# Six w_down blocks rounded among the up projection's weight factors instead of amid w_o's products

## The chip, the cores and the metric

The kernel runs on one core of one Trainium2 chip. The metric is the device time of one execution in microseconds (us). The engines are named as in the profile: PE multiplies matrices, with PEld for its weight loads; ACT, DVE and POOL work element by element; SP issues transfers. Transfers issued by SP and by POOL are shown there as two queues, q1 (hardware_dynamic) and q0 (software_dynamic). A transfer of POOL can add into its destination.

## The reference

One encoder layer for 512 tokens of width 2048, all in float32. Cut to what matters here:

```python
h = rms_norm(x, pre_mix_g)
z = h @ w_in
a = chunked_attention(q, k, v, rel_bias)
p = multiscale_pool(u, pool_w, pool_scale)
m = concatenate([a, p], axis=-1) @ w_o            # 2048 x 2048
x = x + rms_norm(m, post_mix_g)
h = rms_norm(x, pre_ffn_g)
up = causal_dwconv(h @ w_up, conv_w, conv_b)      # 2048 x 11264
y = (gelu(up[..., :F]) * up[..., F:]) @ w_down    # 5632 x 2048
x = x + rms_norm(y, post_ffn_g)
```

## The kernel before

**Numbers in two halves.** PE works on a format shorter than float32, so each operand is split: `split(hi, lo, src)` has ACT round the source into `hi` (L140) and DVE subtract to get the rest `lo` (L141). A product takes three matmuls for each pair of tiles (`mm3`, L162 to L165), or two in `mm2` (L170 wide, L176 narrow).

**Seven products for eight.** The large matrices are multiplied in 2 x 2 blocks by a scheme of seven products of sums of blocks, numbered 1 to 7. The sums of weight blocks are made by transfers that add, either in DRAM beforehand or into a raw tile in on-chip memory.

**Stages.** First come the projections by `w_in` and attention, then w_o's products (414.7 to 523 us in the profile shown), then the norm and the first up blocks, then the loop of the up projection (some 620 to 1416 us), then the down projection, which ends in the last norm and the output.

**w_o's products.** `wo_product(i, cc, ...)` does product i on column half cc in four quarters, each with a weight tile of 128 x 1024 from `weights.get`, which keeps loads and splits running ahead. After each quarter of every product but the first it steps a generator, `ready_blocks`, which prepares six blocks of 128 x 1024 of `w_down` (three factors, two parts each, listed in `ready_parts`). For each block it loads the raw values into `rw` by SP (L843), four steps later splits them into `rwh` and, in place, `rw`, one step later stores both halves to the DRAM tiles `ready_w` by SP (L850), and waits three steps. Both tiles have one buffer each in pool p2, so a block's load waits for the stores of the one before. 48 steps make the six blocks. The stage also adds products into y, sums squares (`junk`, L910), multiplies by the gain (L915), makes the norm's factor (L952 to L955) and updates x (L967).

**The up projection's loop.** 41 column blocks k with seven products each, 287 in all. `Factors` holds a list of entries `(k, i)`, in which products of neighbouring k are interleaved: in one round of seven stand 1 of k, 6 of k-1, 2 of k, 7 of k-1, 5 of k, 4 of k-1, 3 of k. `load` fetches a raw tile by SP (L1345) some nine entries before its use. `make` splits it into a pair `wfh`, `wfl` of the ring w4 (eight buffers, so four pairs), and then has POOL add another weight block into the raw tile (L1362): after products 1, 5 and 6 into wx, after 3 into wy. The result is the raw tile of the entry four places later in the list of products (5, 6, 4 and 7). `get` is called before each product and keeps three entries made ahead of the one in use:

```python
            def get(self, n=AHEAD):
                self.used += 1
                self.prefetch(0)
                self.prefetch(n)
                v, self.made[self.used - 1] = self.made[self.used - 1], None
                return v
```

Behind a product, `keep` copies its accumulator out: ACT copies 1 into za (L1412), 5 into zb (L1418), 6 into zm (L1422), 7 into zm (L1426). Products 1, 6, 7 and 4 of one k share an accumulator bank, and so do 5 and 3, so that 7 cannot begin before the copy of 6 is done. When a k is complete, ACT and DVE do the convolution taps (L1206 to L1208) and gelu (L1220), or the gated product (L1230), which POOL stores as gd (L1233).

**Order.** PE's order is the order of the program. The instructions of the other engines, SP's and POOL's transfers too, are put into a fixed order for each engine when the kernel is built, by a scheduler that goes by priorities and estimated times; on the chip each of these queues is worked off in that order, and an instruction that waits holds those behind it. A call of `tc.issue_after` fixes single pairs.

**Use of the ready blocks.** `right`, at the start of the down projection, loads `ready_w` by POOL (L1110) for the products (0, 1), (1, 1) and (0, 2) of its first chunk.

Of the kernel before, what the change touches and what calls it, by code (L numbers as in the profile page):

```python
# [9 lines left out]
F32 = mybir.dt.float32  # L10
F32R = mybir.dt.float32r
# [4 lines left out]
P = 128  # L16
# [14 lines left out]
PLAIN = 3  # L31
CU = 4
AHEAD = 3
SCALE = 1.0 / math.sqrt(DH)
PAD = 16
WIDE = S + 64
# [9 lines left out]
def f32(ap):  # L46
    return ap.bitcast(F32)
# [34 lines left out]
def encoder_layer(ctx: ExitStack, tc: tile.TileContext, x, xT, vecs, rel, post_mix, post_ffn,  # L82
# [7 lines left out]
    nc = tc.nc  # L90
# [21 lines left out]
    def raw4(name):  # L112
        return big.tile([P, 1024], F32, tag="raw", bufs=5, name=name)

    def w4(name):
        return big.tile([P, 1024], F32R, tag="w4", bufs=8, name=name)
# [21 lines left out]
    def split(hi, lo, src, scale=None):  # L138
        if scale is None:
            rounded = nc.scalar.activation(hi, src, AF.Copy)  # L140
            rest = nc.vector.tensor_sub(lo, src, f32(hi))  # L141
        else:
            rounded = nc.scalar.activation(hi, src, AF.Copy, scale=scale)
            rest = nc.vector.scalar_tensor_tensor(lo, src, scale, f32(hi), op0=ALU.mult, op1=ALU.subtract)
        split.last, split.rest = rounded.ins, rest.ins
        return rounded.ins
# [109 lines left out]
    def first_block(cc, j, l):  # L256
        cs = slice(l * D // 2 + cc * S, l * D // 2 + (cc + 1) * S)
        return w_down[:2 * P * CU, cs].rearrange("(u j p) n -> p u j n", j=2, p=P)[:, :, j, :]

    READY = (0, 1), (1, 1), (0, 2)  # L260
    ready_w = {at: [dram.tile([P, CU, S], F32, name=f"rw{at[0]}{at[1]}{p}") for p in "hl"] for at in READY}

    ready_parts = [(at, j) for at in READY for j in range(2)]
# [88 lines left out]
    for kb in range(KD):  # L352
        i, o = divmod(kb, 8)
# [79 lines left out]
    class Pairs:  # L433
# [25 lines left out]
        def make(self, k, i):  # L459
            if k is None:  # L460
                weights.prefetch_to(FIRST_PART + 1)
                self.made.append(None)
                return
            x, w, y, z = (self.raw.get((k, what)) for what in "xwyz")
            hi, lo = w4("wfh"), w4("wfl")
            split(hi, lo, {3: y, 7: y, 2: z}.get(i, x))
            if i == 1:
                nc.vector.tensor_add(x, x, w)
            elif i == 5:
                nc.vector.tensor_add(x, x, y)  # L470
            elif i == 6:
                nc.vector.tensor_add(x, x, z)
            elif i == 3:
                nc.vector.tensor_add(y, y, w)
            self.made.append(tuple(v.rearrange("p (a b) -> p a b", a=8) for v in (hi, lo)))
# [13 lines left out]
        def get(self):  # L489
            while self.order[self.used][0] is None:  # L490
                self.used += 1
            self.used += 1
            self.prefetch(self.AHEAD)
            v, self.made[self.used - 1] = self.made[self.used - 1], None
            return v
# [117 lines left out]
    with tc.tile_pool(name="p1", bufs=2, reuse_waits="tile") as p1:  # L613
# [222 lines left out]
                split(*(w[:, 4 * i:4 * i + 4, :] for w in parts), v)  # L836
            return parts

        def ready_blocks():
            for at, j in ready_parts:  # L840
                v, hi = (p2.tile([P, 1024], dt, tag=tag, name=tag) for tag, dt in (("rw", F32), ("rwh", F32R)))
                lo = v.bitcast(F32R)
                nc.sync.dma_start(v.rearrange("p (a b) -> p a b", a=2),  # L843
                                  first_block(at[0], at[1] - 1, 0)[:, 2 * j:2 * j + 2, :])
                for _ in range(4):
                    yield
                split(hi, lo, v)
                yield
                for dest, part_ in zip(ready_w[at], (hi, lo)):
                    nc.sync.dma_start(dest[:, 2 * j:2 * j + 2, :], f32(part_).rearrange("p (a b) -> p a b", a=2))  # L850
                for _ in range(3):
                    yield

        ready_steps = ready_blocks()

        wo_banks = [bank(f"m{n}") for n in range(8)]
        ONTO = 6, 3, 7, 4

        def wo_product(i, cc, left, between=None):
            at = 2 * cc + (4 if i in (2, 5, 3) else 0)  # L860
            ps = wo_banks[at:at + 2]
            for q in range(4):
                w = weights.get(f"wo{i}_{cc}_{q}")
                for j in range(2):
                    kb = 2 * q + j
                    for t in range(2):
                        mm3(ps[t], tuple(v[:, kb, t * P:(t + 1) * P] for v in left), part(w, j),
                            i not in ONTO and kb == 0, kb == 7, i in ONTO)
                if i != 1:
                    next(ready_steps, None)  # L870
                if between:
                    between(q)
            return ps
# [328 lines left out]
    with tc.tile_pool(name="p3", bufs=2, reuse_waits="tile") as p3:  # L1202
# [119 lines left out]
        class Factors:  # L1322
# [3 lines left out]
            def __init__(self):  # L1326
                n = 2 * NU - PLAIN

                self.alone = 0, n - 1
                place_of = {1: 0, 6: 8, 2: 2, 7: 10, 5: 4, 4: 12, 3: 6}
                begin = [(0, 1), (0, 2), (0, 5), (1, 1), (0, 3)]
                end = [(n - 1, 5), (n - 2, 6), (n - 1, 3), (n - 1, 1), (n - 2, 7), (n - 1, 6), (n - 2, 4),
                       (n - 1, 7), (n - 1, 2), (n - 1, 4)]
                order = sorted((7 * k + at, k, i) for k in range(n) for i, at in place_of.items())
                self.order = begin + [(k, i) for _, k, i in order if (k, i) not in begin + end] + end
                self.raw, self.made, self.loaded, self.used = {}, [], 0, 0

            def block(self, k, m, kh):  # L1340
# [2 lines left out]
            def load(self, k, i):  # L1343
                def raw(what, tile_, m, kh):
                    nc.sync.dma_start(tile_, self.block(k, m, kh))  # L1345
                    self.raw[k, what] = tile_

                if i == 1 and (k, "w") not in self.raw:
                    raw("w" if k in self.alone else "x", raw4("wx") if k == self.alone[0] else raw_x("wx"), 0, 0)
                elif i == 5 and k == self.alone[0]:  # L1350
                    raw("x", raw4("wx"), 0, 0)
                    self.add(k, "x", 1, 0)
                elif i == 5 and k == self.alone[1]:
                    raw("w", raw_x("wx"), 0, 0)
                    raw("x", raw_x("wx"), 1, 0)
                elif i == 3:
                    raw("y", raw4("wy"), 1, 1)
                elif i == 2:
                    raw("z", raw4("wz"), 0, 1)
# [2 lines left out]
                nc.gpsimd.dma_start(self.raw[k, what], self.block(k, m, kh), accum_op=ALU.add)  # L1362

            def make(self, k, i):
                what = {1: "w" if k in self.alone else "x", 3: "y", 7: "y", 2: "z"}.get(i, "x")
                v = self.raw[k, what]
                if (k, i) == (self.alone[1], 5):
                    nc.vector.tensor_add(v, v, self.raw[k, "w"])
                hi, lo = w4("wfh"), w4("wfl")
                split(hi, lo, v)  # L1370
                if len(self.made) == 2:
                    self.third = split.last, split.rest
                if i == 1 and k not in self.alone:
                    self.add(k, "x", 1, 0)
                elif i == 5:
                    self.add(k, "x", 1, 1)
                elif i == 6:
                    self.add(k, "x", 0, 1)
                elif i == 3:
                    self.add(k, "y", 1, 0)  # L1380
                self.made.append(tuple(v.rearrange("p (a b) -> p a b", a=8) for v in (hi, lo)))
# [6 lines left out]
                    self.make(*self.order[len(self.made)])  # L1388

            def get(self, n=AHEAD):  # L1390
                self.used += 1
                self.prefetch(0)
                self.prefetch(n)
                v, self.made[self.used - 1] = self.made[self.used - 1], None
                return v
# [76 lines left out]
            r = rights[cc].send(i)  # L1472
            firsts.append((firsts[0][0] if firsts else first_left(), r))

        for k, i in factors.order:
            seven(k, i)
            keep(k, i)
            if (k, i) == factors.order[0]:
                with ExitStack() as behind:
                    for ins in factors.third:  # L1480
                        behind.enter_context(tc.issue_after(ins))
                    h_difference()
            if (k, i) == (0, 6):
                with tc.issue_after(keep.six):
                    gates[1] = gate(1, z)
            if (k, i) == (end, 6):
                summed.close()
                pr = ctx.enter_context(tc.tile_pool(name="pr", bufs=2, side="right", reuse_waits="tile"))
            if (k, i) == (end, 6):
                next_first()  # L1490
            elif (k, i) == (end - 1, 4):
                next_first()
# [252 lines left out]
```

## Time and profile before

| what | value |
|---|---|
| time, median of 3 runs | 1864.02 us (1860.69 to 1864.48) |
| the profiled execution | 1858.89 us |
| its span, first to last instruction | 1857.1 us |
| rounding of one ready block, ACT / DVE | 1.06 us / 1.23 us |
| ready blocks: first load issued, last split | 415.3 us, 507.0 us |
| from issue to landing, adds into wx on POOL, median | 6.2 us |
| ACT's waits for rw's loads | 17.1 us in 5 waits, longest 5.8 us |

A line of the profile names the source line, the engine, the operation and the tiles (out<-in), then the count, the busy time and what ended the idle time before it. A timeline's rows start with the start and the duration in us; what stands in brackets at the end is how long the engine had been idle and what it waited for. Rows of DMA issues show the issuing queue; their duration is that of the issue, not of the transfer. Times of single rows belong to the profiled execution.

### The profile page before, as it was taken

The numbers are of one execution on the slowest core, as the hardware profiler recorded it, in microseconds if no ns is written. First come the engines' busy times: TensorE is split into PE (matmuls) and PEld (weight loads), VectorE is DVE, ScalarE is ACT, GpSimd is POOL, SyncE is SP. The second block draws the span as 40 slices with busy tenths as digits, with TensorE's granted clock in tenths as the row PEclk, the third lists the DMA queues.
The fourth block names the chain that finished last, engine by engine and source line by source line (L and its number), as shares of the span: only waits on it lengthen the run. The fifth ranks groups of instructions, "written<-read, shape, count | busy, mean of one in ns | idle before, by whom it ended". The sixth has DMA issues, their size and how long they took to land.

```text
span 1857.1 us, 25452 instructions
## 1 busy us (share of the span) xinstructions
PE 1842.6 (99%) x9598; PEld 1584.3 (85%) x9598; DVE 1532.2 (83%) x1799; ACT 1084.4 (58%) x1376; POOL 302.8 (16%) x402
## 2 busy tenths in 40 slices
PE   9999999999999999999999999999999999999998
PEld 7888888888879888888888888888888888888886
DVE  6988778878588988888887888888887899899876
ACT  7654455456564666566565665666655655565553
POOL 3411001100000112212122122121121001111101
PEclk9999999999999999999999999999999999999999
DMA  8599977998987798888888988889888977777785
GB/s 319 171 319 302 322 230 233 267 264 310 326 308 202 185 220 195 205 204 200 201 200 203 207 202 195 204 206 205 199 179 288 363 224 171 193 211 178 176 230 157
DMA packets 139338, 426.01 MB, mean 229 GB/s; under 512 B 11920, under 2 KB 15376, under 8 KB 133520
## 3 DMA queue, kind: packets, MB, share of 16 engines
q0 software_dynamic: 54864, 173.56, 45.8%
q1 hardware_dynamic: 84352, 250.84, 38.8%
q8 instruction: 75, 1.23, 0.3%
q14 instruction: 47, 0.39, 0.1%
HBM read 370.35 MB, written 104.33 MB: 256 GB/s over the span
## 4 chain that ended last, share of the span: by engine, by line
PE 69%; DMA 1%; DVE 1%; issue 0%; ACT 0%; DVEq 0%; POOLq 0%; ACTq 0%
PE qa L170 16%; PE qa L176 8%; PE qg L170 8%; PE qg L176 4%; PE qd L170 4%; PE pa L162 4%; PE pa L165 4%; PE pa L164 4%; PE qd L176 2%; PE pg L162 2%; PE pg L165 2%; PE pg L164 2%; PE up L165 1%; PE up L162 1%; PE up L164 1%; PE pd L164 1%
## 5 line engine op out<-in xcount | busy, mean ns | idle before, releaser
L140 ACT ACTIVATE wfh<-wx 128x1024 fp32r<-128x1024 f32 x192 | 203.4, 1059 | 154.3 <-PE qg L170 54.4
L170 PE MATMUL qa<-gT,wfh 128*128 128x512 f32 x1152 | 288.6, 392 | 0.0
L141 DVE TENSOR_TENSOR wfl<-wx,wfh 128x1024 fp32r<-128x1024 f32 x192 | 234.6, 1222 | 61.0 <-ACT wfh L140 44.0
L170 PEld LDWEIGHTS qa<-gT,wfh 128*128 128x128 f32 x1152 | 207.2, 189 | 37.1
L1362 POOL DMA_DIRECT2D wx<-in_w_up x122 | 104.6, 858 | 502.6 <-DVE wfl L141 467.9
L140 ACT ACTIVATE wfh<-wy 128x1024 fp32r<-128x1024 f32 x96 | 101.7, 1060 | 108.5 <-PE qg L170 57.2
L170 PE MATMUL qg<-h,wfh 128*128 128x512 f32 x656 | 162.2, 389 | 0.1
L176 PE MATMUL qa<-gT,wfl 128*128 128x256 f32 x1152 | 161.4, 283 | 0.6 <-ACT zm L1422 0.6
L176 PEld LDWEIGHTS qa<-gT,wfl 128*128 128x128 f32 x1152 | 151.5, 191 | 4.9 <-ACT zm L1422 0.8
L170 PEld LDWEIGHTS qg<-h,wfh 128*128 128x128 f32 x656 | 122.9, 188 | 25.9 <-ACT zb L1418 0.5
L141 DVE TENSOR_TENSOR bl<-b,bh 128x2048 fp32r<-128x2048 f32 x56 | 127.2, 2285 | 19.1 <-ACT bh L140 11.7
L140 ACT ACTIVATE bh<-b 128x2048 fp32r<-128x2048 f32 x56 | 106.0, 1911 | 52.8 <-DVE b L1126 21.8
L141 DVE TENSOR_TENSOR wfl<-wy,wfh 128x1024 fp32r<-128x1024 f32 x96 | 117.1, 1220 | 12.6 <-ACT wfh L140 7.8
L162 PE MATMUL pa<-bh,ah 128*128 128x512 f32 x320 | 124.5, 389 | 0.0
L164 PE MATMUL pa<-bl,ah 128*128 128x512 f32 x320 | 124.5, 389 | 0.0
L165 PE MATMUL pa<-bh,al 128*128 128x512 f32 x320 | 124.5, 389 | 0.0
L141 DVE TENSOR_TENSOR wfl<-wz,wfh 128x1024 fp32r<-128x1024 f32 x48 | 58.7, 1223 | 54.2 <-PE qa L170 54.2
L176 PEld LDWEIGHTS qg<-h,wfl 128*128 128x128 f32 x656 | 89.5, 190 | 6.4
L170 PE MATMUL qd<-gT,wfh 128*128 128x512 f32 x384 | 94.9, 389 | 0.0
L176 PE MATMUL qg<-h,wfl 128*128 128x256 f32 x656 | 91.5, 282 | 0.0
L170 PEld LDWEIGHTS qd<-gT,wfh 128*128 128x128 f32 x384 | 71.9, 188 | 14.9
L170 PE MATMUL qa<-h,wfh 128*128 128x512 f32 x328 | 82.1, 392 | 0.0
(554 smaller groups left out, 4352.5 us busy)
## 6 DMA issues: line engine op xcount, KB each, us to landing
wx<-in_w_up POOLq DMA_DIRECT2D x122, 512.0 KB, 6.2
b<-in_w_down SPq DMA_DIRECT2D x32, 1024.0 KB, 7.0
wt<-in_w_o POOLq DMA_DIRECT2D x24, 1024.0 KB, 16.8
wx<-in_w_up SPq DMA_DIRECT2D x43, 512.0 KB, 5.5
wz<-in_w_up SPq DMA_DIRECT2D x41, 512.0 KB, 5.7
wy<-in_w_up SPq DMA_DIRECT2D x41, 512.0 KB, 4.7
wy<-in_w_up POOLq DMA_DIRECT2D x41, 512.0 KB, 6.7
sum<-part POOLq DMA_DIRECT2D x38, 512.0 KB, 6.4
```

Of the source, the lines that this page charges most:

```text
L140: rounded = nc.scalar.activation(hi, src, AF.Copy)
L141: rest = nc.vector.tensor_sub(lo, src, f32(hi))
L162: nc.tensor.matmul(ps, l[0], r[0], start=first, stop=False, skip_group_check=onto)
L164: nc.tensor.matmul(low, l[0], r[1], start=False, stop=False, skip_group_check=onto)
L165: nc.tensor.matmul(ps, l[1], r[0], start=False, stop=last, skip_group_check=onto)
L170: nc.tensor.matmul(ps, w[0][:, kb], pairs[kb][0], start=fresh and not kb, stop=last, skip_group_check=not fresh)
L176: nc.tensor.matmul(ps[:, sl], w[1][:, kb], pair[:, sl], start=False, stop=last, skip_group_check=not fresh)
L1362: nc.gpsimd.dma_start(self.raw[k, what], self.block(k, m, kh), accum_op=ALU.add)
```

## The change

The generator `ready_blocks`, its two tiles and its steps in `wo_product` are removed. In their place six entries `(None, at)` are put into the list of `Factors`, at places 60, 84, 108, 132, 156 and 180 of the list, so in front of the real products 60, 83, 106, 129, 152 and 175 (counted from 0). For such an entry `load` fetches the raw block into a buffer of the ring raw4 (five buffers, shared with wy and wz), and `make` splits it into a pair of the ring w4 and stores both halves by SP. `get` passes over the entry, and the loop over the products leaves it out.

```diff
+READY_FROM, READY_EVERY = 60, 24
...
-        def ready_blocks():
-            for at, j in ready_parts:
-                v, hi = (p2.tile([P, 1024], dt, tag=tag, name=tag) for tag, dt in (("rw", F32), ("rwh", F32R)))
-                lo = v.bitcast(F32R)
-                nc.sync.dma_start(v.rearrange("p (a b) -> p a b", a=2),
-                                  first_block(at[0], at[1] - 1, 0)[:, 2 * j:2 * j + 2, :])
-                for _ in range(4):
-                    yield
-                split(hi, lo, v)
-                yield
-                for dest, part_ in zip(ready_w[at], (hi, lo)):
-                    nc.sync.dma_start(dest[:, 2 * j:2 * j + 2, :], f32(part_).rearrange("p (a b) -> p a b", a=2))
-                for _ in range(3):
-                    yield
-
-        ready_steps = ready_blocks()
...
-                if i != 1:
-                    next(ready_steps, None)
...
+                for at in range(len(ready_parts)):
+                    self.order.insert(READY_FROM + READY_EVERY * at, (None, at))
...
-                if i == 1 and (k, "w") not in self.raw:
+                if k is None:
+                    at, j = ready_parts[i]
+                    v = self.raw[k, i] = raw4("rw")
+                    nc.sync.dma_start(v.rearrange("p (a b) -> p a b", a=2),
+                                      first_block(at[0], at[1] - 1, 0)[:, 2 * j:2 * j + 2, :])
+                elif i == 1 and (k, "w") not in self.raw:
...
             def make(self, k, i):
+                if k is None:
+                    at, j = ready_parts[i]
+                    parts = w4("rwh"), w4("rwl")
+                    split(*parts, self.raw[k, i])
+                    for dest, v in zip(ready_w[at], parts):
+                        nc.sync.dma_start(dest[:, 2 * j:2 * j + 2, :], f32(v).rearrange("p (a b) -> p a b", a=2))
+                    self.made.append(None)
+                    return
...
             def get(self, n=AHEAD):
+                while self.order[self.used][0] is None:
+                    self.used += 1
                 self.used += 1
...
-        for k, i in factors.order:
+        for k, i in [at for at in factors.order if at[0] is not None]:
```

## The prediction

> **What bounds the kernel now.** I read the page first, then TensorE's waits, then a table of stretches, then the timelines around the two places that the change touches.
>
> ```profile
> span 1857.1 us, 25452 instructions
> ...
> PE 1842.6 (99%) x9598; PEld 1584.3 (85%) x9598; DVE 1532.2 (83%) x1799; ACT 1084.4 (58%) x1376; POOL 302.8 (16%) x402
> ...
> PEclk9999999999999999999999999999999999999999
> ```
>
> PE is busy for 99% of the span at a clock that is never lowered, so what can be won is idle time of PE: 14.5 us in all, start and end of the kernel included. PE's own waits say where:
>
> ```profile
> PE m L164 <- DVE wo_1l L141: 2.7, 1, 2.7
> ...
> PE pd L164 <- DMA bl<-rw02l: 0.6, 1, 0.6
> PE qa L176 <- ACT zm L1422: 0.6, 1, 0.6
> ```
>
> One wait of 2.7 us lies in w_o's products, one of 0.6 us in the up projection's loop. The table of stretches shows the loop (1000 to 1100) and w_o's stage (414.7 to 523; columns: length, then busy us of PE, PEld, DVE, ACT, POOL, clock, DMA share, GB/s):
>
> ```profile
> 1000.00:1100.00 100.00, 100.00 (x574) 88.20 (x573) 82.43 (x97) 60.19 (x74) 22.65 (x27) 1.00 0.88 203
> ...
> 414.70:523.00 108.30, 105.60 (x470) 87.21 (x469) 81.38 (x78) 64.88 (x79) 0.72 (x1) 1.00 0.88 307
> ```
>
> The loop has no idle PE at all in such a stretch; the stage that the blocks leave has 2.7 us. That is nearly all that this change can win.
>
> **The change, part by part.** *What goes from w_o's stage.* The wait of 2.7 us ends a chain that begins with the last block (ACT rows, then DVE, then PE):
>
> ```profile
> 499.02 1.06 ACT L140 ACTIVATE wo_2h<-wo_2r 128x1024 fp32r<-128x1024 f32 x1 [1.09 <-PE m L164]
> 505.93 1.06 ACT L140 ACTIVATE rwh<-rw 128x1024 fp32r<-128x1024 f32 x1 [5.84 <-DMA rw<-in_w_down]
> 506.89 1.05 ACT L140 ACTIVATE wo_3h<-wo_3r 128x1024 fp32r<-128x1024 f32 x1
> ...
> 508.58 0.64 ACT L910 ACTIVATE junk<-y 128x512 f32<-128x512 f32 x1
> ```
> ```profile
> 501.29 1.37 DVE L906 TENSOR_TENSOR y<-m,y 128x512 f32<-128x512 f32 x2
> 507.02 1.23 DVE L141 TENSOR_TENSOR rw<-rw,rwh 128x1024 fp32r<-128x1024 f32 x1 [4.36 <-ACT rwh L140]
> ...
> 509.34 1.23 DVE L915 TENSOR_TENSOR y<-y,gain 128x1024 f32<-128x1024 f32 x1
> ...
> 512.86 4.86 DVE L967 SCALAR_TENSOR_TENSOR x<-y,small,x 128x1024 f32<-128x1024 f32 x4
> 517.64 1.21 DVE L141 TENSOR_TENSOR wo_1l<-wo_1r,wo_1h 128x1024 fp32r<-128x1024 f32 x1
> ```
> ```profile
> 518.91 0.50 PE L164 MATMUL m<-wo_1l,s 128*128 128x512 f32 x1 [2.70 <-DVE wo_1l L141]
> ```
>
> ACT sits 5.84 us before the rounding of rw, whose load is late; the squares (junk) that the norm needs stand behind it, then come the gain, four x updates of 4.86 us together, and only then wo_1l. Without the block the squares need only y, ready at 501.29 + 1.37 = 502.7. With wo_3h before them (1.05) they end near 505.2 in place of 509.2, so all behind moves up some 4 us. PE wanted wo_1l 2.70 us before 518.91: the wait goes whole, with about 1.3 us to spare. **Minus 2.7 us.** What is late next there is nothing: PE has no other wait in the stage. The other five roundings, their 12 engine steps and 18 DMAs were covered by PE's own work and give nothing back. That the pool loses 8 KB of tiles is costed at nothing, since PE has no wait where the next pools begin; its price if a buffer moves badly is open, and its nearest row is the 0.6 us wait.
>
> *What comes into the loop: engine time.* Seven products make one round; the same line one round apart stands here, from the chain that ended last:
>
> ```profile
> 655.26 1.91 PE qa L176 x16
> ...
> 674.76 1.91 PE qa L176 x16
> ```
>
> 19.50 / 7 = 2.785 us for a product. The six blocks come 24 entries apart, 23 products or 64 us. Each adds 1.06 us to ACT and 1.23 us to DVE (rows at 505.93 and 507.02); ACT is busy 60% and DVE 82% of the loop, so 64 us leave 25 and 11 us free. Cost nothing, as long as nothing is queued behind.
>
> *DMA work.* Per block one load and two stores of 512 KB. Of the queues,
>
> ```profile
> q0 software_dynamic: 54864, 173.56, 45.8%
> q1 hardware_dynamic: 84352, 250.84, 38.8%
> ```
>
> q1 takes 0.388 x 1857.1 / 250.84 = 2.87 us of all 16 engines for a MB: 1.5 us for the load, 3.0 us for the stores. At a share of 0.88 the loop leaves 7.7 us in 64, so the 4.5 us fit on average. SP's queue now has stores that wait for ACT's and DVE's halves, and raw loads stand behind them. Those are early: this wz is used 16 us after its issue (SP, then ACT):
>
> ```profile
> 788.46 0.33 SPq L1345 DMA_DIRECT2D wz<-in_w_up  x1
> ```
> ```profile
> 804.80 1.06 ACT L140 ACTIVATE wfh<-wz 128x1024 fp32r<-128x1024 f32 x1 [0.36 <-PE qa L176]
> ```
>
> Some 3 us behind a store costs nothing there.
>
> *The place in the ring.* Factors live in four pairs of w4 buffers, and a rounding waits until PE is done with the pair four entries back. A block takes one entry, so the three factors after it are made one product, 2.785 us, later. PE itself doesn't feel that. But three factors in seven are followed by an accumulating DMA on POOL, another by one into wy, and each result is wanted four products later. The tightest case recurs every 39 us. Here its factor is rounded, its add issued, and the result rounded by ACT, with gelu (ca) and the copy zm behind it, which PE needs for its next turn in that bank (ACT, POOL, ACT, PE):
>
> ```profile
> 783.39 1.06 ACT L140 ACTIVATE wfh<-wx 128x1024 fp32r<-128x1024 f32 x1 [1.22 <-PE qg L170]
> ...
> 795.19 1.06 ACT L140 ACTIVATE wfh<-wx 128x1024 fp32r<-128x1024 f32 x1 [1.84 <-DMA wx<-in_w_up]
> 796.16 1.04 ACT L1220 ACTIVATE ca<-ca 128x1024 f32<-128x1024 f32 x1
> 797.11 0.57 ACT L1422 ACTIVATE zm<-qa 128x512 f32<-128x512 f32 x1
> ```
> ```profile
> 786.01 0.85 POOL L1362 DMA_DIRECT2D wx<-in_w_up  x1 [1.98 <-DVE wfl L141]
> ```
> ```profile
> 798.07 1.12 PE L176 MATMUL qa<-gT,wfl 128*128 128x256 f32 x8
> ```
>
> Slack: 798.07 - 797.11 - 0.57 = 0.39 us. Counting entries from the loop's first product, the product at 792.51 us is number 61, so the factor rounded at 783.39 is the second behind **block 1** (before number 60) and comes 2.785 us later. If its add lands as much later, ACT is held and zm with it: 2.785 - 0.39 = **2.4 us** of PE. **Block 4** (before number 129) hits the same case with no slack at all:
>
> ```profile
> 991.20 1.06 ACT L140 ACTIVATE wfh<-wx 128x1024 fp32r<-128x1024 f32 x1 [2.07 <-DMA wx<-in_w_up]
> ...
> 993.11 0.58 ACT L1422 ACTIVATE zm<-qa 128x512 f32<-128x512 f32 x1
> ```
> ```profile
> 993.74 1.22 PE L176 MATMUL qa<-gT,wfl 128*128 128x256 f32 x8 [0.58 <-ACT zm L1422]
> ```
>
> Here the 0.58 us wait exists already; 2.785 - 0.05 = **2.7 us** more. Blocks 2, 3, 5 and 6 (before 83, 106, 152, 175) delay factors of other phases, whose results have 2 us and more in hand; I take nothing for them.
>
> How much later the add lands is not shown. Bounds: nothing, if it gains from meeting fewer of its kind (its landing varies widely),
>
> ```profile
> DMA to landing us min/median/max: 4.5/5.9/10.2
> ```
>
> and 2.785 + 3.0 us, if the block's stores stretch it too. I take 2.785, the plain shift of its issue. **Sum:** -2.7 + 2.4 + 2.7 = +2.4 us. The profiled execution took 1858.89 us with a span of 1857.1, so it would be 1861.3; the median shown is 1864.02, 5.1 us higher, and the forecast is **1866.4 us**.
>
> **The rivals.** *Slower, by the stores.* Blocks 3 and 6 put their stores beside the same tight add, without delaying its issue:
>
> ```profile
> 913.36 0.58 ACT L1422 ACTIVATE zm<-qa 128x512 f32<-128x512 f32 x1
> ...
> 1108.85 0.58 ACT L1422 ACTIVATE zm<-qa 128x512 f32<-128x512 f32 x1
> ```
> ```profile
> 915.03 1.12 PE L176 MATMUL qa<-gT,wfl 128*128 128x256 f32 x8
> ...
> 1110.96 1.12 PE L176 MATMUL qa<-gT,wfl 128*128 128x256 f32 x8
> ```
>
> Slack 1.09 and 1.53 us. If an add waits out the whole 3.0 us of stores, PE loses 1.9 and 1.5 us more: +5.8, 1869.8 us. It decides once stores delay an add by over 1.1 us. For it speaks the DMA share of 0.88, against it that PE bore landings of up to 10.2 us with 0.6 us of idle time. [...]
>
> *All hidden.* The adds land early enough, or zm is queued ahead of the late rounding, since the queue order of ACT is set anew: only -2.7 stays, 1861.3 us. The quiet loop speaks for it.
>
> *The stage doesn't gain.* The x updates (4.86 us) still stand before wo_1l and PE still waits: 1869.1 us. Against it stands the 1.3 us to spare.
>
> *Faster.* The timed runs are 5.1 us above the profiled one. If that sits in later rw loads, the change takes it too: 1861.3 - 5.1 = 1856.2 us. Nothing shown places it there.
>
> **How the numbers follow.** Forecast 0.36, stores 0.27, all hidden 0.20, no gain in the stage 0.05, faster 0.12. A measurement can tell about 0.2%, 3.7 us. Within it lie the forecast and the hidden case: 0.56. Slower: 0.27 + 0.05 = 0.32. Faster: 0.12. The range reaches from under the hidden case to over the stores' one, 1859.5 to 1871.0, and leaves out the last rival and the tails; the likeliest case alone would have 1863 to 1868.
>
> **What would show it.** Right: no wait of PE on wo_1l; in the loop waits of qa L176 on zm near the first and fourth block, 2 to 3 us each, behind a longer wait of ACT on wx. Wrong: no such waits (hidden), waits at the third and sixth (stores), a wait on wo_1l still there, or PE waiting for wfh itself or for SP's loads, which I cost at nothing.

## The result, and the profile after

| | before | after |
|---|---|---|
| median (range, runs) | 1864.25 us (1860.69 to 1865.52, 4) | 1880.76 us (1878.46 to 1885.15, 4) |
| profiled execution, span | 1858.89 us, 1857.1 us | 1880.22 us, 1878.5 us |

The ratio is 1.0094, 95% interval 1.0071 to 1.0118: the change costs 0.9%. The forecast was 1866.4 us, the range ended at 1871.0.

Behind the change the lines of the source have moved a little: the rounding is L141, the subtraction L142, the wide and narrow matmuls of the loop L171 and L177, the adds L1351, the copies of products 6 and 5 L1421 and L1417, the blocks' stores L1359. The page of the changed kernel, and TensorE's waits in it:

```profile
span 1878.5 us, 25469 instructions
...
PE 1849.0 (98%) x9598; PEld 1589.0 (85%) x9598; DVE 1532.3 (82%) x1799; ACT 1081.7 (58%) x1376; POOL 303.5 (16%) x402
```
```profile
PE qa L177 <- ACT zm L1421: 14.2, 10, 5.0
PE qg L171 <- ACT zb L1417: 4.9, 1, 4.9
```

The 2.7 us wait on wo_1l is gone. In its place stand eleven waits in the loop, 19.1 us together, two of them of 5 us. The table of stretches (columns as before): w_o's stage in the changed kernel, then 600 us of the loop in the changed kernel, then the same 600 us in the kernel before:

```profile
414.70:523.00 108.30, 108.30 (x485) 89.67 (x484) 78.81 (x78) 61.97 (x78) 1.57 (x1) 1.00 0.72 238
```
```profile
700.00:1300.00 600.00, 581.72 (x3298) 511.42 (x3298) 480.80 (x565) 353.13 (x434) 123.79 (x148) 0.99 0.89 210
```
```profile
700.00:1300.00 600.00, 599.42 (x3445) 529.22 (x3444) 496.86 (x585) 365.20 (x446) 130.08 (x155) 1.00 0.88 203
```

In w_o's stage PE is now never idle. In the loop its idle time in 600 us went from 0.6 to 18.3 us. DVE and ACT are not busier, and the DMA share rose by one hundredth: no engine has become the bound.

**Block 1 in the timeline.** ACT first (start, duration, and in brackets the idle time and what ended it):

```profile
777.75 1.06 ACT L141 ACTIVATE rwh<-rw 128x1024 fp32r<-128x1024 f32 x1 [0.85 <-PE qa L177]
...
789.10 1.06 ACT L141 ACTIVATE wfh<-wz 128x1024 fp32r<-128x1024 f32 x1 [5.20 <-DMA rw01l<-rwl]
...
798.67 1.06 ACT L141 ACTIVATE wfh<-wx 128x1024 fp32r<-128x1024 f32 x1 [2.67 <-DMA wx<-in_w_up]
799.63 1.04 ACT L1202 ACTIVATE ca<-ca 128x1024 f32<-128x1024 f32 x1
800.58 0.58 ACT L1421 ACTIVATE zm<-qa 128x512 f32<-128x512 f32 x1
```

The same stretch on DVE, on SP, on POOL and on PE:

```profile
786.97 2.36 DVE L142 TENSOR_TENSOR wfl<-wx,wfh 128x1024 fp32r<-128x1024 f32 x2 [4.76 <-DMA rw01h<-rwh]
```
```profile
778.84 0.33 SPq L1359 DMA_DIRECT2D rw01h<-rwh  x1
780.90 0.33 SPq L1359 DMA_DIRECT2D rw01l<-rwl  x1
```
```profile
788.49 0.87 POOL L1351 DMA_DIRECT2D wx<-in_w_up  x1 [8.86 <-DVE wfl L142]
789.62 0.85 POOL L1351 DMA_DIRECT2D wx<-in_w_up  x1 [0.26 <-DVE wfl L142]
```
```profile
801.21 2.08 PE L177 MATMUL qa<-gT,wfl 128*128 128x256 f32 x8 [4.96 <-ACT zm L1421]
803.08 3.12 PE L171 MATMUL qa<-gT,wfh 128*128 128x512 f32 x8
```

Read it from the block on. rwh is rounded at 777.75, its store issued at 778.84; rwl's store at 780.90. Then the engines stop: DVE's next subtraction waits until the store of **rwh** has landed (4.76 us), and ACT's rounding of wz until that of **rwl** has (5.20 us; it starts 8.2 us after that store's issue). These are writes into wfl and wfh, two tiles that have nothing to do with the block. What ties them to its stores is the ring: by these waits, they are given the buffers that rwh and rwl had (the profile itself leaves buffer numbers out). The subtractions hold two adds on POOL; these issue at 788.49 and 789.62. Before, the second of them issued at 786.01, 6.5 us ahead of product 61 on PE (792.51); now it issues 0.9 us ahead of that product (790.52), so it is 5.6 us late. Its value lands too late, so ACT waits 2.67 us for wx; behind that wait stand gelu (ca) and the copy zm, and PE waits 4.96 us for zm. That last part, from the add to PE, is the chain of the prediction; what starts it is another thing. The chain of work that ended last passes through the store itself (start, duration, what):

```profile
779.65 1.24 DVE rwl L142
...
780.90 8.18 DMA rw01l<-rwl
...
789.10 1.07 ACT wfh L141
```

### The profile page after: what moved, and what is told of

Read it like the earlier page. It is cut to its first block, busy times and chain, and to the rows that moved or that the text cites. A ratio compares the mean times of both kernels' runs of the same rounds, so it can differ in the third digit from the quotient of the medians.

```text
span 1878.5 us, 25469 instructions
## 1 busy us (share of the span) xinstructions
PE 1849.0 (98%) x9598; PEld 1589.0 (85%) x9598; DVE 1532.3 (82%) x1799; ACT 1081.7 (58%) x1376; POOL 303.5 (16%) x402
## 4 chain that ended last, share of the span: by engine, by line
PE 90%; DMA 6%; issue 1%; ACT 1%; DVE 1%; SPq 0%; POOL 0%; DVEq 0%; POOLq 0%; ACTq 0%
PE qa L171 16%; PE qa L177 9%; PE qg L171 8%; PE qg L177 4%; PE pa L163 4%; PE pa L166 4%; PE pa L165 4%; PE qd L171 4%; PE m L163 3%; PE m L165 3%; PE m L166 3%; DMA wx<-in_w_up 2%; PE pg L163 2%; PE pg L166 2%; PE pg L165 2%; PE qd L177 2%
## 5 line engine op out<-in xcount | busy, mean ns | idle before, releaser
L141 ACT ACTIVATE wfh<-wx 128x1024 fp32r<-128x1024 f32 x192 | 203.4, 1059 | 165.3 <-PE qg L171 50.8
L142 DVE TENSOR_TENSOR wfl<-wx,wfh 128x1024 fp32r<-128x1024 f32 x192 | 234.6, 1222 | 75.1 <-ACT wfh L141 51.0
L171 PE MATMUL qa<-gT,wfh 128*128 128x512 f32 x1152 | 290.0, 394 | 0.0
L171 PEld LDWEIGHTS qa<-gT,wfh 128*128 128x128 f32 x1152 | 208.5, 190 | 37.4
L1351 POOL DMA_DIRECT2D wx<-in_w_up x122 | 105.2, 862 | 518.7 <-DVE wfl L142 475.7
L177 PE MATMUL qa<-gT,wfl 128*128 128x256 f32 x1152 | 163.1, 285 | 14.2 <-ACT zm L1421 14.2
L177 PEld LDWEIGHTS qa<-gT,wfl 128*128 128x128 f32 x1152 | 152.2, 192 | 20.4 <-ACT zm L1421 16.2
L171 PE MATMUL qg<-h,wfh 128*128 128x512 f32 x656 | 164.1, 393 | 4.9 <-ACT zb L1417 4.9
L141 ACT ACTIVATE wfh<-wy 128x1024 fp32r<-128x1024 f32 x96 | 101.6, 1058 | 106.1 <-PE qg L171 48.1
L171 PEld LDWEIGHTS qg<-h,wfh 128*128 128x128 f32 x656 | 123.8, 189 | 31.3 <-ACT zb L1417 5.6
L142 DVE TENSOR_TENSOR bl<-b,bh 128x2048 fp32r<-128x2048 f32 x56 | 127.2, 2287 | 19.6 <-ACT bh L141 12.0
L141 ACT ACTIVATE bh<-b 128x2048 fp32r<-128x2048 f32 x56 | 106.1, 1913 | 55.4 <-DVE b L1108 22.3
L142 DVE TENSOR_TENSOR wfl<-wy,wfh 128x1024 fp32r<-128x1024 f32 x96 | 117.2, 1221 | 22.8 <-ACT wfh L141 15.8
L142 DVE TENSOR_TENSOR wfl<-wz,wfh 128x1024 fp32r<-128x1024 f32 x48 | 58.8, 1225 | 50.3 <-PE qa L171 39.3
L177 PEld LDWEIGHTS qg<-h,wfl 128*128 128x128 f32 x656 | 90.3, 192 | 6.5
L171 PE MATMUL qd<-gT,wfh 128*128 128x512 f32 x384 | 94.9, 389 | 0.0
L177 PE MATMUL qg<-h,wfl 128*128 128x256 f32 x656 | 92.3, 284 | 0.0
L171 PEld LDWEIGHTS qd<-gT,wfh 128*128 128x128 f32 x384 | 72.0, 188 | 14.8
L171 PE MATMUL qa<-h,wfh 128*128 128x512 f32 x328 | 82.1, 392 | 0.0
```

The source lines that it names most:

```text
L171: nc.tensor.matmul(ps, w[0][:, kb], pairs[kb][0], start=fresh and not kb, stop=last, skip_group_check=not fresh)
L177: nc.tensor.matmul(ps[:, sl], w[1][:, kb], pair[:, sl], start=False, stop=last, skip_group_check=not fresh)
```

## The experiments

All ratios are to the kernel before, run on the same chip beside them. The theory after the comparison: *the hold*. A block's w4 pair goes back to the ring only when its stores have landed, and the loop cannot spare it that long. Rivals: *the place* (the prediction's: the pair takes an entry of the ring, so what follows is late), *the work* (the rounding, the subtraction, the load and the stores themselves), *the phase* (where in the round of seven products the blocks fall).

**Other buffers.** The halves go into raw buffers; loads, stores, engine steps and places in the list are those of the change.

```diff
-                    parts = w4("rwh"), w4("rwl")
-                    split(*parts, self.raw[k, i])
+                    v = self.raw[k, i]
+                    parts = raw4("rwh").bitcast(F32R), v.bitcast(F32R)
+                    split(*parts, v)
```

> The changed kernel, but a block's two halves don't take buffers of the ring w4: hi goes to a buffer of the raw ring, lo stands in place over the raw block. Theory A (buffers: the halves sit in w4 buffers until their stores land, and the next factors are given just these buffers): no ACT or DVE wait on a store of rw is left, PE's waits in the loop fall from 19.1 us to under 3 us, time 1861 to 1867 us. Theory B (traffic: the stores and loads slow the adding transfers): PE's waits stay above 10 us, time 1875 us or more. Theory C (the prediction's: a block takes a place in the ring, so three factors and their adds come one product later): here no place in the ring is taken either, so 1861 to 1867 us as for A.

Measured: 1861.49 us (1858.06 to 1864.55, 10 runs), ratio 0.9999 [0.9986, 1.0011]. TensorE's waits in the loop:

```profile
PE qa L177 <- ACT zm L1422: 4.5, 5, 1.9
...
PE qg L171 <- ACT zb L1418: 0.5, 1, 0.5
```

Nearly the whole loss goes away with the buffers; of 19.1 us of waits 5.0 are left. No wait of ACT or DVE on a block's store remains. The work, traffic included, costs about the 2.7 us that w_o's stage gives (0.1 to 4.7 us by the interval). One thing more differs: the splits don't wait for a w4 buffer and come earlier. Block 1's rounding starts at 767.18 us, 23.5 us ahead of product 61 on PE (790.72), in place of 12.8 us in the changed kernel. The next run speaks to that.

**The parts of the work by themselves**, in the kernel before, with its blocks in w_o's stage left as they are. First the loads and splits again in the loop, into w4, the results stored nowhere; then the loads and two stores of the raw values to spare DRAM tiles, with no split and no w4.

```diff
+                if k is None:
+                    parts = w4("rwh"), w4("rwl")
+                    split(*parts, self.raw[k, i])
+                    self.made.append(None)
+                    return
```

> The kernel before (its ready blocks stay amid w_o's products), with six further blocks loaded and split in the loop at the places of the change, in w4 buffers, and not stored: the place in the ring and the engine time without stores. Theory A: without stores nothing holds the buffers, so the loop gains no long waits: before plus 0 to 3 us, 1864 to 1867 us. Theory B: only six loads are added, before plus 0 to 2 us. Theory C: PE's waits of 2 to 3 us each at the first and fourth block, before plus 5 us, 1869 us.

```diff
+                if k is None:
+                    at, j = ready_parts[i]
+                    v = self.raw[k, i]
+                    for dest in spare_w[at]:
+                        nc.sync.dma_start(dest[:, 2 * j:2 * j + 2, :], v.rearrange("p (a b) -> p a b", a=2))
+                    self.made.append(None)
+                    return
```

> The kernel before, with six blocks loaded into raw buffers in the loop at the places of the change and stored twice each to spare DRAM, nothing split and no w4 buffer taken: the DMA traffic alone. Theory A: before plus 0 to 4 us, 1864 to 1868 us. Theory B: before plus 15 us or more, 1879 us. Theory C: before plus 0 to 3 us.

Measured: 1866.59 us, ratio 1.0023 [1.0004, 1.0042], and 1866.8 us, ratio 1.0024 [1.0011, 1.0036]. Either costs some 4 us; neither, nor the two together, comes near the change. A pair of w4 without stores is cheap, and so are stores without w4.

The first of these two runs, with splits into w4 and no stores, also answers the earlier splits above: block 1's rounding starts at 784.84 us, again 12.8 us ahead of product 61 (797.61). The second add behind it issues at 791.85, 5.8 us ahead of that product, and PE waits 0.64 us for zm. Before, it was 6.5 us. So place, rounding and moment together make this add 0.7 us late; with the stores it is 5.6 us late, and PE waits 4.96 us.

**One half held, the other not.**

```diff
-                    parts = w4("rwh"), w4("rwl")
-                    split(*parts, self.raw[k, i])
+                    v = self.raw[k, i]
+                    parts = w4("rwh"), v.bitcast(F32R)
+                    split(*parts, v)
```

> The changed kernel with hi in a w4 buffer and lo in place over the raw block: one w4 buffer for each block is held by a store in place of two. Theory A: waits on the store of hi alone stay, and the loss against the kernel before falls to between a quarter and three quarters: 1866 to 1876 us. Theory of sums: the traffic is the same and half a place is left, 1874 us or more.

Measured: 1874.08 us (1868.96 to 1881.74, 6 runs), ratio 1.0068 [1.0043, 1.0092]. With none, one and two buffers held: 0.9999, 1.0068, 1.0094. The one half that is held is the one that is waited for (who waited for rwh, and how long its stores took):

```profile
  ACT wfh L141: 10.8, 2
  DVE wfl L142: 6.4, 4
...
DMA to landing us min/median/max: 5.7/6.5/8.4
```

**Place, work and phase taken together or doubled.** Five runs; the edits are to the version with raw buffers unless said. A second split into a w4 pair that nobody reads or stores:

```diff
+                    split(w4("dwh"), w4("dwl"), v)
```

> As e1, and each block is split a second time into a pair of w4 buffers that nothing reads and nothing stores: the place in the ring, the traffic and twice the engine time together, but no store on a w4 buffer. Theory A (w4 buffers are held until a store lands and given to the very next factors): 1862 to 1869 us, no wait on a store. Theory of sums (B and C together, place plus traffic plus engine time make the loss, the stores' hold on the buffers nothing): 1876 us or more, as the changed kernel.

Measured: 1873.67 us (1867.68 to 1875.24, 6 runs), ratio 1.0056 [1.0036, 1.0077]. That lies in neither of the two ranges. The place looks dear here, but the run also splits twice. So the second split alone, into a raw buffer:

```diff
+                    dummy = raw4("dwh").bitcast(F32R)
+                    split(dummy, dummy, v)
```

> As e5, but the second split goes to a raw buffer: twice the engine time and the traffic, no w4 buffer. It tells apart what e5 lost against e1 (12 us). If w4 buffers are what costs, 1860 to 1865 us as e1; if the second split's 1.06 us of ACT and 1.22 us of DVE for each block cost it, 1870 us or more.

Measured: 1874.79 us (1871.63 to 1883.59, 6 runs), ratio 1.0067 [1.0039, 1.0095], the same as with the place. ACT's waits for added tiles, in this run and then with raw buffers alone:

```profile
ACT wfh L141 <- DMA wx<-in_w_up: 40.5, 29, 2.5
...
ACT wfh L141 <- DMA wy<-in_w_up: 29.8, 9, 5.2
```
```profile
ACT wfh L141 <- DMA wx<-in_w_up: 39.0, 26, 3.8
...
ACT wfh L141 <- DMA wy<-in_w_up: 10.7, 5, 2.9
```

And the third raw buffer alone, cleared in 8 columns, to part it from the engine time:

```diff
+                    nc.vector.memset(raw4("dwh")[:, :8], 0.0)
```

> The changed kernel with the halves in raw buffers, and beside them one further raw buffer per block that is only touched by a small clearing of 8 columns on DVE and read by nothing. It tells apart the two things that the run with the second split in a raw buffer added (1874.8 us): 3.5 us more of engine time per block, and a third buffer of the raw ring. If the engine time cost there, this run stays at 1860 to 1864 us. If the third raw buffer cost, by pushing the later raw loads or the block's own a buffer back, it goes to 1870 to 1876 us, with waits of PE qa on zm of 10 us and more in sum.

Measured: 1863.22 us (1859.19 to 1871.56, 12 runs), ratio 1.0012 [0.9997, 1.0027]. The 3.5 us per block of the expectation are 1.06 us of ACT and 1.22 us of DVE in the rows. So the second split's 12 us are put down to engine time: one split per block passes, a second at the same spot does not. (It also holds its buffer a little longer than the clearing does, which no run parts from it.) The run with the place had shown nothing of the place.

**The place alone**, then. A w4 pair is taken and 8 columns of each tile cleared; no hold, no second split. At the changed kernel's places, and at places 42 products apart (`READY_FROM, READY_EVERY = 32, 43`), where every block falls ahead of the tight add:

```diff
+                    for tag in ("dwh", "dwl"):
+                        nc.vector.memset(f32(w4(tag))[:, :8], 0.0)
```

> The changed kernel with the halves in raw buffers, and beside them a pair of w4 per block of which only 8 columns are cleared on DVE, read by nothing and stored nowhere: the pair's place in the ring without a hold and without a second split. If the place costs what the prediction gave it (2.4 us at block 1 and 2.7 at block 4), 5 us over the run with raw buffers alone: 1865 to 1869 us, with waits of PE qa on zm near products 62 and 132. If the hold alone is what costs, 1860 to 1864 us and no wait over 2 us there. If the place is most of the 19 us, 1872 us and more.

> The same at places 32, 43, where raw buffers alone gave 1856.0 us and w4 buffers 1881.9. If the hold is what costs, 1855 to 1860 us; if each block's place costs 2.8 us in this tight phase, 6 x 2.8 = 17 us more, 1870 to 1875 us; the prediction's 2.5 us would be reached only where no slack is there, so about 1863 to 1870 us by its own slack of 0.4 to 1.5 us.

Measured: 1859.16 us, ratio 0.9994 [0.9980, 1.0008], and 1861.97 us, ratio 1.0008 [0.9995, 1.0021]. TensorE's waits of the two:

```profile
PE qa L177 <- ACT zm L1424: 3.0, 7, 0.7
```
```profile
PE qa L177 <- ACT zm L1424: 2.1, 3, 1.0
```

At the changed kernel's places, the place in the ring costs nothing that can be measured. At 32, 43 the run lies between its ranges, some 6 us over the one with raw buffers alone (0.9972 [0.9955, 0.9988], table below), and the waits of the two profiles, 2.1 and 1.1 us, don't account for it.

**The phase, and the distance of the blocks.** The halves in raw buffers with `READY_FROM, READY_EVERY` of 68, 29 (the calm part of the round), of 60, 29 and of 32, 43 (the tight part); the changed kernel's w4 with 68, 29 and 32, 43.

> As e1, with the blocks at places 68, 97, 126, 155, 184, 213 of the list, so 28 products apart and always in the part of the two-column rhythm where no three adding transfers lie close together. Theory A: 1860 to 1863 us, PE's waits in the loop at most 1 us, since the 2.7 us of w_o's stage are won and no store meets a tight add. Theory B: lower than e1 by most of what e1 loses. Theory C: as e1.

> As e1 and e4, with the blocks at places 60, 89, 118, 147, 176, 205, so 28 products apart and always where three adding transfers lie close together and the copy zm has the least slack. Theory A: the phase matters little without a hold on w4 buffers, 1859 to 1864 us. The prediction's rival on stores (they slow the tight add): PE waits on zm of 1 to 2.5 us at most of the six blocks, 1866 to 1873 us.

> The changed kernel, halves in w4 buffers as there, at the places of e4 (68, 97, 126, 155, 184, 213), the calm part of the rhythm. Theory A: ACT or DVE waits on the stores at all six blocks all the same, and 8 us or more are lost against e4: 1868 to 1880 us. Theory C (only adds in the tight part matter): 1860 to 1864 us.

> As e7 (raw buffers, tight part of the rhythm), with the blocks 42 products apart in place of 28 (places 32, 75, 118, 161, 204, 247). If each block still costs PE something by its traffic in the rounds after it, wider spacing gains 1 to 2 us against e7: 1856 to 1858 us. If what e7 has left is the loop's own, the same as e7, 1857 to 1861 us.

> The changed kernel with its blocks 42 products apart (places 32, 43), halves in w4 as in the changed kernel: the same places as the run with 32, 43 and raw buffers (1856.0 us). If the hold of the w4 pair until the stores land is what costs, each block still stalls the loop by about 3 us whatever its distance from the next: 6 x 3 = 18 us over 1856, so 1870 to 1876 us, with waits of ACT or DVE on stores of rw. If the blocks cost because they stood too near one another (what one delays is not made good before the next), 42 products are enough to make it good: under 1862 us, and no wait on a store longer than 2 us.

| places | raw buffers | w4, held by the stores |
|---|---|---|
| 60, 24 | 1861.49 us, 0.9999 [0.9986, 1.0011] | 1880.76 us, 1.0094 [1.0071, 1.0118] |
| 68, 29 | 1859.61 us, 0.9992 [0.9979, 1.0004] | 1878.78 us, 1.0090 [1.0062, 1.0117] |
| 60, 29 | 1858.53 us, 0.9984 [0.9969, 0.9999] | |
| 32, 43 | 1856.03 us, 0.9972 [0.9955, 0.9988] | 1881.92 us, 1.0107 [1.0086, 1.0128] |

In the three rows with both, the buffers make 19, 19 and 26 us by the medians (18, 18 and 25 by the ratios); at 32, 43 that is more than the 14 to 20 us expected. Neither phase nor distance saves the ring: at 32, 43 with w4, six waits on zm make 15.2 us, one for each block, and behind them are again waits for stores (TensorE's, then ACT's waits, then the landing of rwl's stores):

```profile
PE qa L177 <- ACT zm L1421: 15.2, 6, 4.4
```
```profile
ACT wfh L141 <- DMA rw02l<-rwl: 8.7, 2, 4.8
ACT wfh L141 <- DMA rw11l<-rwl: 8.6, 2, 4.5
ACT wfh L141 <- DMA rw01l<-rwl: 8.4, 2, 4.3
```
```profile
DMA to landing us min/median/max: 6.9/7.2/7.8
```

With raw buffers and 32, 43 the kernel beats both: 1856.03 us (1854.69 to 1860.36, 10 runs), 0.28% under before. Its loop has one wait on zm:

```profile
PE qa L177 <- ACT zm L1422: 1.1, 1, 1.1
```

## Why the prediction was wrong

*W_o's stage: right.* The wait of 2.7 us went whole, PE is busy for all of 414.7 to 523.

*The step that failed* is the sentence "a rounding waits until PE is done with the pair four entries back". That is when the pair of a product comes free. A block's pair has no product; it comes free when its two stores have landed. So the shift behind a block was priced at one product, 2.785 us. The stores of rwl in the changed kernel took:

```profile
DMA to landing us min/median/max: 4.6/6.9/9.9
```

And the buffers go not to the entry four places on, but to halves of the next three factors, which are wanted at once: behind block 1 the low half of the first or second (the row at 786.97) and the high half of the third (789.10). The prediction named the stores as DMA work and as traffic beside an add, never as readers that hold a ring buffer. The rows that could have shown it stood in its reach: the landing of a DMA, 4.5 to 10.2 us, beside one product of 2.785 us.

*What it gave to blocks 1 and 4* (2.4 and 2.7 us) it gave to the place in the ring; the place alone costs nothing at these places (0.9994 against 0.9999). Even with the rounding, it made block 1's add 0.7 us late and not 2.785, and PE's waits behind the two blocks were 0.64 and 0.68 us (0.58 of the second stood there before). That the two longest waits, 5.0 and 4.9 us, fall behind these very blocks is luck: another cause put them there. For block 4, ACT:

```profile
993.21 1.06 ACT L141 ACTIVATE wfh<-wx 128x1024 fp32r<-128x1024 f32 x1 [5.59 <-DMA rw11l<-rwl]
995.87 1.06 ACT L141 ACTIVATE wfh<-wx 128x1024 fp32r<-128x1024 f32 x1 [1.60 <-DMA rw11l<-rwl]
996.83 0.58 ACT L1417 ACTIVATE zb<-qg 128x512 f32<-128x512 f32 x1
```

Here no late add is needed: the copy zb stands behind the held roundings, and PE waits for it at once.

*Blocks 2, 3, 5 and 6 at nothing: wrong.* Of the other nine of the eleven waits two small ones stand ahead of the first block; seven, of 2.1, 1.0, 1.2, 1.7, 0.8, 0.2 and 1.3 us, come 9 to 50 us after these blocks' roundings, 8.4 us in sum; not each of them is traced to a store. At 32, 43 with w4 every block stalls the loop.

*Engine time at nothing: nearly*, for one split: with raw buffers the loop has 5.0 us of waits in place of 0.6, and that includes the traffic. The condition put with it ("as long as nothing is queued behind") is what a second split breaks.

*DMA work at nothing: nearly.* Loads and stores alone cost 0.24% [0.11, 0.36], some 4 us with w_o's blocks still there; with raw buffers they and the rest are made good by the 2.7 us (ratio 0.9999).

*From late add to PE: right* as a mechanism, in the rows 798.67 to 801.21. That the add lands as late as it issues was right too: ACT starts on its value 9.1 us after the issue, before 9.2 us.

*The price of a wait* was its own length. The sum of the span is: 19.1 us of waits in the loop in place of 0.6, the 2.7 us of w_o's stage and 0.6 on bl gone, +15.2; the span grew by 21.4. About 5 us of the rest are slow matmuls after the two long waits (next section); some 1 us is not placed.

*The rivals.* Stores stretching an add (1869.8) is not what came: its price came from stores beside adds, and stores without the hold cost little. That PE would wait for its factors was listed as what would prove it wrong; PE doesn't, it waits for the copies behind them.

It stays open why the place alone costs some 6 us at 32, 43 (1856.03 without, 1861.97 with it) when it costs nothing at 60, 24. That a store that lands sooner would cure the ring was not tried.

## What to carry to other kernels

A ring buffer is paid for by its last reader, and a store here was a reader until it had landed (the row at 789.10): before a piece of work takes a slot of a ring that runs at the pace of products, compare that landing time (here 4.6 to 9.9 us) with the ring's step (2.785 us). Put what is only prepared and stored into a ring with slack, or into its own input buffer; here the same work then cost about what its removal from w_o's stage gave. And an engine that is 60% busy may still have no room at one spot of its queue: ask what copy for PE stands behind the new instruction.

## What the runs showed of the hardware

**Two waits of PE cost more than their length.** After the waits of 4.96 and 4.91 us PE ran slower for a while. Block 4, PE, and the stretches at and behind both waits:

```profile
997.46 3.78 PE L171 MATMUL qg<-h,wfh 128*128 128x512 f32 x8 [4.91 <-ACT zb L1417]
1001.04 1.91 PE L177 MATMUL qg<-h,wfl 128*128 128x256 f32 x8
1002.74 2.34 PE L171 MATMUL qa<-gT,wfh 128*128 128x512 f32 x8
1004.92 1.11 PE L177 MATMUL qa<-gT,wfl 128*128 128x256 f32 x8
```
```profile
801.00:809.00 8.00, 7.79 (x34) 6.87 (x35) 4.94 (x6) 3.70 (x5) 1.29 (x2) 0.72 0.82 178
...
997.00:1005.00 8.00, 7.54 (x25) 6.38 (x26) 5.93 (x7) 4.09 (x6) 0.85 (x1) 0.60 0.94 200
1005.00:1013.00 8.00, 8.00 (x52) 7.26 (x51) 6.57 (x9) 5.50 (x7) 0.85 (x1) 1.00 0.60 132
```

Eight matmuls of 512 columns took 3.78 us in place of some 2.0, eight of 256 1.91 in place of 1.11: (3.78 - 2.0) + (1.91 - 1.11) + (2.34 - 2.0) = 2.9 us here, and (2.08 - 1.11) + (3.12 - 2.0) = 2.1 us after the first wait, 5.0 together. The granted clock of these 8 us is 0.72 and 0.60, then 1.00 again; it was 0.50 for 6.8 us each time, from 798.67 to 805.49 and from 996.64 to 1003.46. PE was busy for 4.28 and 6.00 us of these stretches. With the loads and stores alone, slow matmuls followed a wait of 2.75 us as well (granted clock 0.66 from 518 to 523 us),

```profile
511.92 0.39 PE L163 MATMUL m<-wo_3h,s 128*128 128x512 f32 x1
...
519.45 0.80 PE L165 MATMUL m<-wo_1l,s 128*128 128x512 f32 x1 [2.75 <-DVE wo_1l L142]
520.04 0.63 PE L166 MATMUL m<-wo_1h,s 128*128 128x512 f32 x1
```

0.63 us for a matmul that took 0.39 ahead of the wait, while behind the 2.70 us wait of the kernel before the clock stayed at 1.00:

```profile
518.90:521.90 3.00, 2.99 (x16) 2.49 (x16) 3.00 (x4) 0.39 (x1) 0.00 (x0) 1.00 0.92 325
```

So of two waits of nearly the same length, 2.75 and 2.70 us, one was followed by slow matmuls and the other was not. What decides it was not shown.

**The same store lands at another time.** rwh's stores, 512 KB each, at the same places and with the same transfers, with raw buffers and then in the changed kernel:

```profile
DMA to landing us min/median/max: 2.6/4.0/5.7
```
```profile
DMA to landing us min/median/max: 5.6/6.3/8.5
```

The stores issue at other moments in the two kernels (rwh's first at 768.3 and at 778.84 us); what makes the difference was not tried. In the changed kernel ACT waited 8.1 us in three waits and DVE 4.8 us in one for rwh's stores to land; with raw buffers nothing waited for them.
